# Who copies four partial sums out of PSUM: ScalarE or VectorE, in the gate and up projections of a streaming encoder layer

## The chip, the cores and the metric

The kernel runs on one core of a Trainium2 chip. The metric is the device time of one execution in microseconds (us); the median over runs is compared. A core has five engines that work side by side, each with its own in-order queue of instructions: TensorE (PE in the profile; the loading of its weights is shown apart as PEld), VectorE (DVE), ScalarE (ACT), GpSimd (POOL) and SyncE (SP, which here only starts DMAs). Matmuls add up into PSUM, which has eight banks; ScalarE and VectorE read the sums from there into SBUF. Weights come from HBM by DMA.

## The reference

One layer of a hybrid encoder for 320 positions (256 of a new stream, 64 of a running one) that share all weights: RMSNorm, one input projection, stick-breaking attention and a spatial gate, two branch projections, a merge, an output projection, and then the part that the change touches, the feed-forward network:

```
h = x + merged @ w_out[l]
hn = rmsnorm(h, norm_ffn[l])
gu = hn @ w_gate_up[l]
h = h + (jax.nn.silu(gu[..., :D_FF]) * gu[..., D_FF:]) @ w_down[l]
```

All is float32, with D_MODEL = 2048 and D_FF = 5632.

## The kernel before, in words

**Two numbers for one.** Every float32 weight is split in two: `wh`, the weight as ScalarE casts it to the fast matmul type, and `wl`, what is left of it, which VectorE gets by a subtraction (lines 70 and 71 in the projections before and after; lines 554 and 555 in the gate and up projections). Activations are split in the same way. A product then is high by high, high by low and low by high.

**The feed-forward network** goes over the 5632 hidden features in three slices of 16, 16 and 12 blocks of 128 (line 681). In a slice, `quad` (line 542) computes four blocks at a time, first for the gate half of the weights, then for the up half, so that there are 8, 8 and 6 quads, 22 in all; behind the quads of a slice the down projection for that slice runs (lines 687 to 698). Below, a quad for the gate half is a gate quad and one for the up half an up quad, and tile 0 to tile 7 are the eight pieces of weight (two rows of blocks by four columns, 512 KB each) that a quad loads.

**One quad** has two phases on TensorE:

- The main phase: for each of the eight tiles, SyncE loads `raw` (line 546; three buffers), ScalarE casts it into `wh` (line 554; four buffers), VectorE subtracts into `wl` or `low` (line 555; nine buffers, of which one quad uses eight), and ten matmuls 512 columns wide (line 562) use `wh` as the moving operand, 80 in all. They add up in three PSUM banks, `main`: the pool `acc` for a gate quad (three banks), the pool `aux` for an up quad (four banks). This result lies turned, with positions on the partitions.
- The low phase: four blocks b = 0 to 3 of 16 matmuls each (line 572), with the low parts of the weights as the stationary operand, each block summing in a bank of its own. Blocks 0 and 2 use the pool `aux1`, which has a single bank; blocks 1 and 3 take a bank of `aux`. **Line 573** copies the sum of a block (128 by 320) into the SBUF tile `total`, and so frees its bank. Block 2 can only begin when the copy of block 0 is done, as both use the one bank of `aux1`.

**Turning the main result** (`quad_turn`, line 580) is called ahead of the low phase: for each of the two 16-bit halves (planes) of the float32 numbers ScalarE makes three copies out of the `main` banks (line 587) and issues a transposing DMA (line 588). `quad_join` (line 591) is due some steps later: VectorE puts the two turned planes together (line 594, twice; the first needs both planes to have landed), adds them to `total` (lines 596 and 597), and then comes `gate_out` (lines 601 and 602) or `up_out` (lines 606 to 611).

**The order of the work** comes from a tile scheduler, which puts each engine's instructions in an order of its own from what it thinks they cost. It starts the casts and subtractions of the next quad inside the low phase of this one. `later` and `at` hold steps back until a given tick of the program; `quad_join` is due five ticks after the main phase.

**Who waits for whom.** A `raw` buffer is loaded again when both its cast and its subtraction are done. A `wl` or `low` buffer comes free when block 3 has used it, since block 3 is the last that reads it. So VectorE can subtract only one tile of the next quad before block 3 begins.

## Time and profile before

| what | value |
|---|---|
| median of three runs | 1700.63 us (1700.49 to 1702.84) |
| the profiled execution's own time | 1699.94 us |
| its span (first to last instruction) | 1698.2 us |
| TensorE busy | 1681.7 us, 99% |
| VectorE busy | 935.4 us, 55% |
| ScalarE busy | 769.4 us, 45% |
| granted TensorE clock, mean | 0.998 |

The profile is one execution. A row of a group tells the line, the engine, the operation, the tiles written and read, how many, their busy time, the mean of one in ns, and the idle time of that engine ahead of them with what ended it. A timeline row begins with the start and the length in us; xN says that N instructions are put together in it, and the brackets at its end show the idle time ahead of it and what released it. "ACTq" is the issuing of a DMA by ScalarE's queue.

### The profile page before, as it was taken

What the parts mean: (1) busy time and instruction counts of PE and PEld (TensorE: products, weight loads), DVE (VectorE), ACT (ScalarE), POOL (GpSimd) and SP (SyncE); (2) the same over time, 40 slices, a digit from 0 to 9 for tenths busy, and PEclk for the clock granted to TensorE, in tenths of its full rate; (3) what the DMA queues carried; (4) which work ended last, traced back from release to release, by engine and by line L of the source; (5) the groups of instructions that cost most, each with busy time, mean ns of one, the idle gap of its engine ahead of it and who ended that gap; (6) DMA issues with size and microseconds to landing.
All of it is one profiled execution on the core that took longest, in us unless ns stands there. A gap on an engine that the chain in (4) does not pass through costs nothing.

```text
span 1698.2 us, 25709 instructions
## 1 busy us (share of the span) xinstructions
PE 1681.7 (99%) x10496; PEld 1605.8 (95%) x10496; DVE 935.4 (55%) x1173; ACT 769.4 (45%) x1044; POOL 38.8 (2%) x68
## 2 busy tenths in 40 slices
PE   9999999999999999999999999999999999999998
PEld 9999999999999999998888899988888999888997
DVE  7665656544444445555555554446564644464666
ACT  7555645433333333445545532354555323545443
POOL 1100001000000000000000000000000000000000
PEclk9999999999999999999999999999999999999999
DMA  7866555444444444556666654566566545665554
GB/s 280 261 179 176 158 163 166 116 151 151 149 149 150 149 149 163 173 165 191 167 185 173 182 156 149 153 180 180 170 186 177 159 149 162 171 182 166 157 156 124
DMA packets 236983, 285.50 MB, mean 168 GB/s; under 512 B 98081, under 2 KB 194337, under 8 KB 236865
## 3 DMA queue, kind: packets, MB, share of 16 engines
q1 hardware_dynamic: 164016, 257.72, 48.5%
q10 hardware_dynamic: 70224, 17.88, 6.0%
q0 software_dynamic: 2624, 8.26, 1.6%
q8 instruction: 82, 1.34, 0.3%
q14 instruction: 37, 0.30, 0.0%
HBM read 256.03 MB, written 5.51 MB: 154 GB/s over the span
## 4 chain that ended last, share of the span: by engine, by line
PE 87%; DVE 5%; DMA 3%; ACT 3%; issue 2%; ACTq 0%; SPq 0%; DVEq 0%
PE acc L87 18%; PE acc L89 18%; PE acc L88 18%; PE aux L562 12%; PE aux L572 8%; PE acc L562 4%; DMA raw<-w_gu 3%; PE aux L89 2%; PE aux L88 2%; PE aux L87 2%; ACT flat L587 2%; DVE flat L594 1%; DVE wl L555 1%; DVE low L555 1%; ACT wh L554 1%
## 5 line engine op out<-in xcount | busy, mean ns | idle before, releaser
L70 ACT CAST wh<-raw 128x1024 fp32r<-128x1024 f32 (+2 forms) x296 | 302.7, 1023 | 542.8 <-PE acc L88 390.6
L71 DVE TENSOR_TENSOR wl<-raw,wh 128x1024 fp32r<-128x1024 f32 (+2 forms) x296 | 351.6, 1191 | 247.0 <-ACT wh L70 228.5
L87 PE MATMUL acc<-A,wh 128*128 128x320 f32 x1088 | 337.5, 310 | 0.5 <-ACT A L108 0.5
L88 PE MATMUL acc<-A,wh 128*128 128x320 f32 x1088 | 336.4, 309 | 0.0
L89 PE MATMUL acc<-A,wl 128*128 128x320 f32 x1088 | 336.2, 309 | 0.0
L554 ACT CAST wh<-raw 128x1024 fp32r<-128x1024 f32 x176 | 185.0, 1053 | 207.6 <-DMA raw<-w_gu 85.2
L87 PEld LDWEIGHTS acc<-A,wh 128*128 128x128 f32 x1088 | 204.3, 188 | 2.4 <-issue 1.5
L88 PEld LDWEIGHTS acc<-A,wh 128*128 128x128 f32 x1088 | 204.3, 188 | 0.3 <-DVE A L110 0.3
L89 PEld LDWEIGHTS acc<-A,wl 128*128 128x128 f32 x1088 | 204.2, 188 | 0.4 <-DVE wl L71 0.4
L562 PE MATMUL acc<-wh,A 128*128 128x512 f32 x880 | 201.6, 389 | 0.0
L562 PE MATMUL aux<-wh,A 128*128 128x512 f32 x880 | 201.5, 389 | 0.0
L555 DVE TENSOR_TENSOR low<-raw,wh 128x1024 fp32r<-128x1024 f32 x96 | 117.3, 1234 | 152.6 <-PE aux L572 121.6
L562 PEld LDWEIGHTS acc<-wh,A 128*128 128x128 f32 x880 | 164.7, 188 | 33.8
L562 PEld LDWEIGHTS aux<-wh,A 128*128 128x128 f32 x880 | 164.7, 188 | 33.7
L89 PE MATMUL acc<-act,wl 128*128 128x320 f32 x500 | 154.3, 309 | 0.7 <-DVE wl L71 0.7
L88 PE MATMUL acc<-act,wh 128*128 128x320 f32 x500 | 154.5, 309 | 0.0
L87 PE MATMUL acc<-act,wh 128*128 128x320 f32 x500 | 154.5, 309 | 0.0
L555 DVE TENSOR_TENSOR wl<-raw,wh 128x1024 fp32r<-128x1024 f32 x80 | 97.1, 1221 | 98.6 <-PE aux L572 75.5
L572 PE MATMUL aux<-A,low 128*128 128x320 f32 x768 | 130.6, 310 | 4.6 <-ACT sum L573 4.6
L572 PEld LDWEIGHTS aux<-A,low 128*128 128x128 f32 x768 | 117.2, 188 | 7.5 <-ACT sum L573 6.5
L572 PE MATMUL aux<-A,wl 128*128 128x320 f32 x640 | 110.4, 309 | 1.7 <-ACT sum L573 1.7
L572 PEld LDWEIGHTS aux<-A,wl 128*128 128x128 f32 x640 | 98.3, 188 | 2.9 <-ACT sum L573 2.2
(221 smaller groups left out, 2234.6 us busy)
## 6 DMA issues: line engine op xcount, KB each, us to landing
raw<-w_gu SPq DMA_DIRECT2D x176, 512.0 KB, 3.6
raw<-w_in SPq DMA_DIRECT2D x141, 512.0 KB, 3.7
raw<-w_down SPq DMA_DIRECT2D x80, 512.0 KB, 3.6
raw<-w_out SPq DMA_DIRECT2D x32, 512.0 KB, 3.6
raw<-w_a SPq DMA_DIRECT2D x16, 512.0 KB, 3.5
raw<-w_b SPq DMA_DIRECT2D x16, 512.0 KB, 3.5
raw<-w_down SPq DMA_DIRECT2D x16, 256.0 KB, 2.8
xr<-xT POOLq DMA_DIRECT2D x16, 160.0 KB, 2.5
```

The source lines that it names most:

```text
L70: nc.scalar.copy(out=wh[:, : n * P], in_=raw[:, : n * P])
L71: nc.vector.tensor_tensor(out=wl[:, : n * P], in0=raw[:, : n * P], in1=wh[:, : n * P].bitcast(F32), op=ALU.subtract)
L87: nc.tensor.matmul(ps[:, :T], a, x[0], start=first, stop=False)
L88: nc.tensor.matmul(ps[:, :T], a, x[1], start=False, stop=False)
L89: nc.tensor.matmul(ps[:, :T], b, x[0], start=False, stop=last)
L554: nc.scalar.copy(out=wh, in_=raw)
L555: nc.vector.tensor_tensor(out=wl, in0=raw, in1=wh.bitcast(F32), op=ALU.subtract)
L562: nc.tensor.matmul(main[i // 2].rearrange("p (b m) -> p b m", b=4), x[:, at0 : at0 + P], w, start=k == 0 and i % 2 == 0, stop=k == KD - 1 ...
L572: nc.tensor.matmul(ps[:, :T], lows[k // 2][:, at0 : at0 + P], hg[k][0], start=k == 0, stop=k == KD - 1)
L587: tc.keep_in_program_order(nc.scalar.copy(out=planes[:, i, c * 512 : (c + 1) * 512], in_=hw[:, :, 1 - i]))
L594: nc.vector.tensor_copy(rows[:, :, :, :, 1 - i], turned[:, i].rearrange("p (c b) t -> p b c t", c=3))
```

## The change

Line 573 alone is changed: the copy of a block's sum goes from ScalarE's queue to VectorE's.

```
@@ -570,7 +570,7 @@
             for k in range(KD):
                 at0 = (2 * b + k % 2) * P
                 nc.tensor.matmul(ps[:, :T], lows[k // 2][:, at0 : at0 + P], hg[k][0], start=k == 0, stop=k == KD - 1)
-            nc.scalar.copy(out=total[:, b, :], in_=ps[:, :T])
+            nc.vector.tensor_copy(total[:, b, :], ps[:, :T])
             tick()
         at(now + 5, quad_join, total, *turning)
```

There are 88 such copies, four in each of the 22 quads. The scheduler makes new orders for TensorE, ScalarE and VectorE from it, in the feed-forward part alone; the orders of GpSimd and SyncE stay as they are.

On TensorE, in the low phase of the third gate quad (the one whose main phase begins at 872.53 us in the profile of before; `aux_8779` is the bank of block 2, and `aux` stands for blocks 0, 1 and 3):

```order
 L572 MATMUL aux<-A,low 128x320 x8
 L572 MATMUL aux<-A,wl 128x320 x8
-L572 MATMUL aux<-A,low 128x320 x7
 L572 MATMUL aux_8779<-A,low 128x320 x8
 L572 MATMUL aux_8779<-A,wl 128x320 x8
-L572 MATMUL aux<-A,low 128x320
+L572 MATMUL aux<-A,low 128x320 x8
 L572 MATMUL aux<-A,wl 128x320 x8
```

Before, the scheduler put seven matmuls of block 3 ahead of block 2; now the blocks follow each other whole.

On ScalarE, from the up quad ahead of that gate quad's low phase to the low phase's end, before (`aux_8743` and `aux_8779` are the banks of blocks 0 and 2):

```order
L610 CAST act<-sum 128x320 x4
L554 CAST wh<-raw 128x1024 x4
L587 COPY flat<-acc 128x512 x3
L554 CAST wh<-raw 128x1024
L588 DMA_TRANSPOSE turned<-flat 128x12x128
L587 COPY flat<-acc 128x512 x3
L573 COPY sum<-aux_8743 128x320
L588 DMA_TRANSPOSE turned<-flat 128x12x128
L573 COPY sum<-aux 128x320
L573 COPY sum<-aux_8779 128x320
L573 COPY sum<-aux 128x320
L554 CAST wh<-raw 128x1024 x2
```

and the same place now:

```order
L610 CAST act<-sum 128x320 x4
L554 CAST wh<-raw 128x1024 x3
L587 COPY flat<-acc 128x512 x3
L554 CAST wh<-raw 128x1024
L588 DMA_TRANSPOSE turned<-flat 128x12x128
L587 COPY flat<-acc 128x512 x3
L554 CAST wh<-raw 128x1024
L588 DMA_TRANSPOSE turned<-flat 128x12x128
L554 CAST wh<-raw 128x1024 x3
```

The four copies are gone from it, and the first three copies of line 587 stand one cast earlier.

On VectorE, at the low phase of the up quad that follows (main phase from 901.12 us; `aux_8965` and `aux_9001` are the banks of its blocks 0 and 2), before:

```order
L555 TENSOR_TENSOR wl<-raw,wh 128x1024 x4
L555 TENSOR_TENSOR low<-raw,wh 128x1024 x2
L594 COPY flat<-turned 128x1536 x2
L555 TENSOR_TENSOR low<-raw,wh 128x1024
L596 TENSOR_TENSOR sum<-flat,sum 128x1280
L555 TENSOR_TENSOR low<-raw,wh 128x1024
L597 TENSOR_TENSOR sum<-flat,sum 128x4x64
```

and now:

```order
L573 COPY sum<-aux_8965 128x320
L573 COPY sum<-aux 128x320
L573 COPY sum<-aux_9001 128x320
L555 TENSOR_TENSOR low<-raw,wh 128x1024
L594 COPY flat<-turned 128x1536
L573 COPY sum<-aux 128x320
L594 COPY flat<-turned 128x1536
L555 TENSOR_TENSOR low<-raw,wh 128x1024
L596 TENSOR_TENSOR sum<-flat,sum 128x1280
L555 TENSOR_TENSOR low<-raw,wh 128x1024
L597 TENSOR_TENSOR sum<-flat,sum 128x4x64
L555 TENSOR_TENSOR low<-raw,wh 128x1024
```

Ahead of block 3's copy and of the second subtraction for the next quad there now stands the first line-594 copy, which waits for both turned planes.

More of the change, by code (lines that the diff above doesn't have):

```diff
@@ L572, in quad @@
                 nc.tensor.matmul(ps[:, :T], lows[k // 2][:, at0 : at0 + P], hg[k][0], start=k == 0, stop=k == KD - 1)
-            nc.scalar.copy(out=total[:, b, :], in_=ps[:, :T])
+            nc.vector.tensor_copy(total[:, b, :], ps[:, :T])
             tick()
```

## The prediction

> **What bounds the kernel now.** I read the page first, then the waits of the feed-forward stretch, then its timeline. The page:

> ```profile
> span 1698.2 us, 25709 instructions
> PE 1681.7 (99%) x10496; PEld 1605.8 (95%) x10496; DVE 935.4 (55%) x1173; ACT 769.4 (45%) x1044; POOL 38.8 (2%) x68
> ```

> TensorE is the bound, so a change that leaves the matmuls alone can win only its gaps. The waits from 770 to 1620 us (total, times, longest):

> ```profile
> PEld aux L572 <- ACT sum L573: 8.7, 9, 1.4
> PEld acc L89 <- DVE wl L71: 0.9, 1, 0.9
> DVE low L555 <- PE aux L572: 121.6, 16, 10.1
> DVE wl L555 <- PE aux L572: 75.5, 14, 10.1
> ```

> The weight loads wait nine times for line 573 and once for a subtraction, and for nothing else. VectorE stands still for up to 10.1 us at a time, until block 3 frees a low tile. One of the nine, in the gate quad at 872.53 us, on the timeline, with two phases of quads that have no wait, from the chain:

> ```profile
> 872.53 18.32 PE L562 MATMUL acc<-wh,A 128*128 128x512 f32 x80
> 891.38 1.05 ACT L554 CAST wh<-raw 128x1024 fp32r<-128x1024 f32 x1 [1.24 <-DMA raw<-w_gu]
> 892.33 1.55 ACT L587 COPY flat<-acc 128x512 uint16<-128x512 uint16 x3
> 893.76 1.07 ACT L554 CAST wh<-raw 128x1024 fp32r<-128x1024 f32 x1
> 893.91 1.46 ACTq L588 DMA_TRANSPOSE turned<-flat  x1
> 895.41 1.56 ACT L587 COPY flat<-acc 128x512 uint16<-128x512 uint16 x3 [0.58 <-ACT wh L554]
> 896.85 0.46 ACT L573 COPY sum<-aux 128x320 f32<-128x320 f32 x1
> 897.36 1.43 PE L572 MATMUL aux<-A,low 128*128 128x320 f32 x8 [0.79 <-ACT sum L573]
> 901.12 18.32 PE L562 MATMUL aux<-wh,A 128*128 128x512 f32 x80
> ```
> ```profile
> 845.16 18.16 PE aux L562 x80
> 975.43 9.38 PE aux L572 x64
> ```

> Undisturbed, a quad is 18.16 + 9.38 = 27.54 us; a low block is 9.38 / 4 = 2.35 us and a main tile 18.16 / 8 = 2.27 us. This quad took 901.12 - 872.53 = 28.59 us, 1.05 more. Its block 0 ended near 872.53 + 18.16 + 2.35 = 893.0, but the copy began at 896.85: ScalarE had a late cast, then line 587, a cast, the issue of the transposing DMA and line 587 again in front of it. TensorE did block 1 and the seven early matmuls of block 3, and then stood until the one bank of `aux1` was free.

> **What is removed.** The nine waits, 8.7 us. I count the weight loads' idle time and not that of the matmuls, since 1.05 us lost here is more than the 0.79 us in the matmul row: the first loads and matmuls behind a gap fill the pipeline again.

> **What is added.** 88 copies on VectorE. The trace has none on that engine; the nearest rows of 128x320 and of a like size are:

> ```profile
> L573 ACT COPY sum<-aux 128x320 f32<-128x320 f32 x88 | 38.3, 435 | 82.4 <-PE aux L572 82.4
> L671 DVE TENSOR_TENSOR h<-acc,h 128x320 f32<-128x320 f32 x26 | 12.8, 492 | 35.3 <-PE acc L89 35.3
> L597 DVE TENSOR_TENSOR sum<-flat,sum 128x256 f32<-128x256 f32 x22 | 9.3, 421 | 0.0
> ```

> So 0.42 to 0.49 us, and I take 0.45: line 671 reads PSUM with as many elements but has a second operand. [...]

> **Where the copies lie.** Copies 0, 1 and 2 fall into VectorE's standstill. Block 0 of the up quad at 901.12 ends at 921.63; VectorE's next row begins at 924.96 after 9.92 us of idling (below), so it is free from 915.04. Copy 0 is done by 922.4 and block 2 begins at 923.97: 1.5 us to spare, where ScalarE's copy came too late. Copy 3 and the new order cost something, as the first line-594 copy now stands ahead of copy 3 and of most subtractions for the next quad, and those free the `raw` buffers. What this does to the gate quad at 928.67, from these rows:

> ```profile
> 923.48 1.44 ACTq L588 DMA_TRANSPOSE turned<-flat  x1
> 924.96 1.23 DVE L555 TENSOR_TENSOR low<-raw,wh 128x1024 fp32r<-128x1024 f32 x1 [9.92 <-PE aux L572]
> 927.16 1.23 DVE L555 TENSOR_TENSOR low<-raw,wh 128x1024 fp32r<-128x1024 f32 x1 [0.97 <-PE aux L572]
> 928.31 1.98 DVE L594 COPY flat<-turned 128x1536 uint16<-128x1536 uint16 x2
> 928.67 16.51 PE L562 MATMUL acc<-wh,A 128*128 128x512 f32 x72
> 930.18 1.21 DVE L555 TENSOR_TENSOR low<-raw,wh 128x1024 fp32r<-128x1024 f32 x1
> 931.16 1.05 ACT L554 CAST wh<-raw 128x1024 fp32r<-128x1024 f32 x1 [1.86 <-PE acc L562]
> 931.31 1.48 DVE L596 TENSOR_TENSOR sum<-flat,sum 128x1280 f32<-128x1280 f32 x1
> 932.71 1.22 DVE L555 TENSOR_TENSOR low<-raw,wh 128x1024 fp32r<-128x1024 f32 x1
> ```
> ```profile
> raw<-w_gu SPq DMA_DIRECT2D x176, 512.0 KB, 3.6
> ```
> ```profile
> 1502.18 5.36 DMA raw<-w_gu
> ```
> ```profile
> DMA to landing us min/median/max: 3.6/3.7/5.4
> ```

> The last row is that of the transposing DMAs of line 588. Now, in the new order: block 3 runs from 926.32, its first tile is free after two matmuls and VectorE starts about 0.5 us later, so tile 1 is subtracted from 927.25 to 928.47 (before: 924.96, helped by block 3's early matmuls). The planes landed at 923.48 + 3.7 = 927.2, so line 594 runs to 929.5, copy 3 to 929.95, line 594 to 930.95, tile 2 to 932.15 (before: 928.39), line 596 to 933.5, tile 3 to 934.7 (before: 931.39), line 597 to 935.1, tile 4 to 936.3 (before: 933.93). Each subtraction lets SyncE load the tile three further on: 3.6 us to the landing, 5.36 at the longest in the chain, and 1.05 for the cast. Tile 5 is ready at 936.8 to 938.6 and TensorE wants it at 928.67 + 5 x 2.27 = 940.0; tile 6 at 939.4 to 941.1 for 942.3; tile 7 at 941.0 to 942.7 for 944.6. Between 1.2 and 3.2 us are left, so the cover holds: nothing. In the profile of before the cast at 931.16 waited for TensorE itself, which is where this slack shows. After a gate quad the new order has two subtractions ahead of copy 3, which is easier still. The low parts of tile 7 are wanted only in block 0, 20 us after the main phase begins.

> The chain does not build up from quad to quad, since VectorE waits again for block 3 in each. Moved on ScalarE: line 587 comes one cast earlier in most gate quads and loses nothing.

> **The one place that loses.** Behind the last quad of all VectorE has line 594 twice and then the first subtraction of the down projection, for which TensorE stands:

> ```profile
> 1599.56 1.99 DVE L594 COPY flat<-turned 128x1536 uint16<-128x1536 uint16 x2 [14.53 <-DMA turned<-flat]
> 1601.42 1.22 DVE L71 TENSOR_TENSOR wl<-raw,wh 128x1024 fp32r<-128x1024 f32 x1
> 1602.69 0.42 PE L89 MATMUL acc<-act,wl 128*128 128x320 f32 x1 [0.68 <-DVE wl L71]
> ```

> In the new order copy 2 stands between the two copies of line 594, so the subtraction comes 0.45 us later: +0.45. The other two slice ends have that first subtraction done ahead of copy 0, as before.

> **The sum**: -8.7 + 0.45 = -8.25 us. Against the profiled execution's own 1699.94 us (its span and 1.74 us around it) this is 1691.7. That execution lay 0.7 below the median of the runs, 1700.63, so for the median I say 1692.4.

> **The rivals.**

> *VectorE's queue starves the loads (slower).* The trace speaks for it in that VectorE is the fuller of the two engines. [...] As a mechanism: the planes land late, line 594 holds copy 3 and the subtractions, tile 6 comes late and TensorE stands in its main phase. It decides from the point where more than the 1.2 us left at tile 6 is gone, that is, where both planes land after about 930 instead of 927.2; the longest landing in the trace, 5.4 us, makes it 928.9. Eight gate quads follow an up quad inside a slice; if each stood 1.5 us, the sum were -8.25 + 12 = +3.75: 1704.4 for the median. Chance 0.09.

> *Copy 0 is late on VectorE too (part of the gain).* Tile 0 of the next quad is subtracted ahead of copy 0; by my times the queue shifts by 2 to 4 us and that subtraction ends about 1 to 3 us before block 0 does, with 2 us more until block 2 begins. If it fails in half of the nine, the gain is 8.25 - 4.35 = 3.9 us: 1696.7. Chance 0.12.

> *The wait only changes its owner (no change).* The third block waits for VectorE as long as it did for ScalarE, through something the trace does not show. Against it: VectorE has no work in that time. 1700.6. Chance 0.05.

> **How the numbers follow.** The forecast has 0.74, with its own range from 1690.8 (8.7 + 0.95, should the slice-end wait go as well, and 0.14 from the median to the lowest run) to 1694.5 (a quarter of the gain lost to small waits in the main phases). To hold 8 in 10 the range takes in the partial gain: 1690.8 to 1697.5. About 0.2%, 3.4 us, is what a measurement can tell from no change here; the partial gain straddles it, mostly above. Faster: 0.74 + 0.09 = 0.83. Same: 0.05 + 0.03 = 0.08. Slower: 0.09.

> **What would show it.** In the profile after, line 572 should wait for line 573 no more; every quad should take 27.54 us from one main phase to the next; copies 0 to 2 should sit in VectorE's idle time, 0.42 to 0.49 us each; casts of tiles 5 to 7 should come later than before but still wait mostly for TensorE; and the wait before line 89 at the last quad should grow from 0.95 to about 1.4 us. It is wrong if line 562 waits for line 554 (the first rival), or if line 572 still waits for line 573, now on VectorE (the second and third).

## The result, and the profile after

| | median | lowest to highest | runs |
|---|---|---|---|
| before | 1700.83 us | 1700.48 to 1702.97 | 10 |
| after | 1693.63 us | 1690.93 to 1701.08 | 10 |

The ratio is 0.9961 [0.9946, 0.9975]: faster by 7.2 us, where 1692.4 us was forecast. The new kernel is also less steady: its runs spread over 10 us, those of before over 2.5. Two later runs of the kernel before, which took 4293 and 4589 us, are left out of the medians below. The profiled execution took 1698.68 us, 5 us more than the median, so its trace shows what is given back near its largest.

The page of after:

```profile
span 1696.9 us, 25604 instructions
L573 DVE COPY sum<-aux 128x320 f32<-128x320 f32 x88 | 43.0, 489 | 157.8 <-PE aux L572 157.8
```

The work has moved as meant: VectorE is busy for 971.8 us in place of 935.4 and ScalarE for 734.1 in place of 769.4, a copy takes 489 ns on VectorE, and VectorE spent 157.8 us idle ahead of them, waiting for the blocks' sums. Now the waits between 770 and 1620 us (total, times, longest), after:

```profile
ACT wh L554 <- DMA raw<-w_gu: 259.9, 103, 8.3
DVE flat L594 <- DMA turned<-flat: 40.6, 18, 4.9
ACT wh L554 <- PE acc L562: 21.9, 15, 4.6
PEld acc L562 <- ACT wh L554: 3.5, 6, 1.0
PEld acc L89 <- DVE wl L71: 3.3, 2, 2.7
PEld aux L572 <- ACT flat L587: 1.4, 2, 1.0
```

and the three rows of before that the first three answer to:

```profile
ACT wh L554 <- DMA raw<-w_gu: 85.2, 51, 3.2
DVE flat L594 <- DMA turned<-flat: 19.4, 5, 14.5
ACT wh L554 <- PE acc L562: 54.7, 39, 3.3
```

The nine waits of line 572 for line 573 are gone; no row of that pair is left. Two new rows of the weight loads stand in their place, and the row of line 89 has grown from 0.9 to 3.3 us. One of the new ones is line 562 waiting for line 554: the mark that the prediction gave for its first rival. The casts wait for the weights three times as long as before and much less for TensorE, so the slack ahead of the main phases has shrunk. (That alone costs nothing: with the join later, below, they wait 219.3 us for the weights, and no main phase is longer.) Counted by the starts of all matmuls in that stretch, as far as they lie further apart than the undisturbed pace of their line, TensorE lost 8.8 us at line 572 and 1.2 at line 89 before, and now 1.4 at line 572, 2.5 at line 562 and 4.9 at line 89 with the matmuls right behind it: 10.0 against 8.9. The difference of 1.1 us agrees about with that of the spans, 1698.2 - 1696.9 = 1.3.

The place where it is given back shows best in the second slice. The timeline of VectorE after, only the first line-594 copy behind each quad:

```profile
1120.81 1.05 DVE L594 COPY flat<-turned 128x1536 uint16<-128x1536 uint16 x1
...
1150.21 1.06 DVE L594 COPY flat<-turned 128x1536 uint16<-128x1536 uint16 x1 [1.78 <-DMA turned<-flat]
...
1180.85 1.98 DVE L594 COPY flat<-turned 128x1536 uint16<-128x1536 uint16 x2 [3.34 <-DMA turned<-flat]
...
1208.43 1.07 DVE L594 COPY flat<-turned 128x1536 uint16<-128x1536 uint16 x1 [4.58 <-DMA turned<-flat]
```

The next main phases begin at 1121.41, 1148.95, 1176.49 and 1204.42 us. Against them the planes are put together at -0.60, +1.26, +4.36 and +4.01 us; before it was between -0.37 and +0.30 at all four. The delay grows over three quads and then stays near 4 us. (From the second quad of the first slice on it lies between 0.5 and 2.5 us, in the third between -0.2 and 1.7, and every quad inside these two takes 27.54 or 27.55 us.) The gate quad from 1204.42 then took 29.31 us in place of 27.54. A little later, at the gate quad from 1261.26, the timeline of all engines after shows the whole loop:

```profile
1253.57 1.05 ACT L554 CAST wh<-raw 128x1024 fp32r<-128x1024 f32 x1 [0.51 <-DMA raw<-w_gu]
1254.52 1.55 ACT L587 COPY flat<-aux 128x512 uint16<-128x512 uint16 x3
1256.06 1.05 ACT L554 CAST wh<-raw 128x1024 fp32r<-128x1024 f32 x1
1257.59 1.56 ACT L587 COPY flat<-aux 128x512 uint16<-128x512 uint16 x3 [0.48 <-ACT wh L554]
1259.18 1.43 ACTq L588 DMA_TRANSPOSE turned<-flat  x1
1261.26 17.23 PE L562 MATMUL acc<-wh,A 128*128 128x512 f32 x71
1264.73 1.05 DVE L594 COPY flat<-turned 128x1536 uint16<-128x1536 uint16 x1 [4.00 <-DMA turned<-flat]
1266.36 1.05 ACT L554 CAST wh<-raw 128x1024 fp32r<-128x1024 f32 x1 [7.21 <-DMA raw<-w_gu]
1266.99 1.22 DVE L555 TENSOR_TENSOR low<-raw,wh 128x1024 fp32r<-128x1024 f32 x1
1271.76 1.05 ACT L554 CAST wh<-raw 128x1024 fp32r<-128x1024 f32 x1 [4.35 <-DMA raw<-w_gu]
1272.86 2.17 PEld L562 LDWEIGHTS acc<-wh,A 128*128 128x128 f32 x10 [0.50 <-ACT wh L554]
```

Read it from the top: a cast that is late and waits for its weights stands ahead of both sets of line-587 copies (the cast between the sets stands there in the kernel before too), so the second plane's DMA is issued at 1259.18, 2.1 us ahead of the main phase instead of the 5.2 us of the prediction's quad. VectorE waits 4.00 us for it, with copy 3 and the subtractions queued behind. These subtractions come late, so the `raw` buffers are loaded late, ScalarE stands 7.21 and 4.35 us for weights, and TensorE for the cast. The casts of the next quad stand in ScalarE's queue ahead of the next line 587, and the circle closes. The DMA itself is slower too: in the six quads from 1148.95 us to the slice end the second plane took 5.0 to 6.1 us from issue to landing, where 3.7 is the median. At the gate quad from 1204.42 it landed 3.9 us into the main phase, at the same quad of before 1.5 us ahead of it; 3.7 us of the difference are the later issue and 1.7 the longer transfer.

### The profile page after: what moved, and what is told of

It reads as the page before. It is cut to its first block, busy times and chain, and to the rows that moved or that the text cites. A ratio compares the mean times of both kernels' runs of the same rounds, so it can differ in the third digit from the quotient of the medians.

```text
span 1696.9 us, 25604 instructions
## 1 busy us (share of the span) xinstructions
PE 1682.7 (99%) x10496; PEld 1607.0 (95%) x10496; DVE 971.8 (57%) x1261; ACT 734.1 (43%) x956; POOL 38.9 (2%) x68
## 4 chain that ended last, share of the span: by engine, by line
PE 87%; DMA 5%; DVE 4%; ACT 2%; issue 1%; ACTq 0%; SPq 0%; DVEq 0%
PE acc L89 18%; PE acc L87 18%; PE acc L88 18%; PE acc L562 9%; PE aux L572 8%; PE aux L562 7%; DMA raw<-w_gu 2%; DMA turned<-flat 2%; PE aux L89 2%; PE aux L88 2%; PE aux L87 2%; ACT flat L587 1%; DVE low L555 1%; DVE flat L594 1%; PE acc L639 1%
## 5 line engine op out<-in xcount | busy, mean ns | idle before, releaser
L71 DVE TENSOR_TENSOR wl<-raw,wh 128x1024 fp32r<-128x1024 f32 (+2 forms) x296 | 351.7, 1191 | 224.4 <-ACT wh L70 223.3
L89 PE MATMUL acc<-A,wl 128*128 128x320 f32 x1088 | 336.3, 309 | 0.0
L554 ACT CAST wh<-raw 128x1024 fp32r<-128x1024 f32 x176 | 185.3, 1054 | 317.8 <-DMA raw<-w_gu 259.9
L89 PEld LDWEIGHTS acc<-A,wl 128*128 128x128 f32 x1088 | 204.3, 188 | 0.2 <-DVE wl L71 0.2
L562 PE MATMUL acc<-wh,A 128*128 128x512 f32 x880 | 203.2, 390 | 1.1 <-ACT wh L554 1.0
L562 PE MATMUL aux<-wh,A 128*128 128x512 f32 x880 | 201.5, 389 | 0.0
L562 PEld LDWEIGHTS acc<-wh,A 128*128 128x128 f32 x880 | 164.2, 188 | 37.0 <-ACT wh L554 3.5
L562 PEld LDWEIGHTS aux<-wh,A 128*128 128x128 f32 x880 | 164.8, 188 | 33.7
L89 PE MATMUL acc<-act,wl 128*128 128x320 f32 x500 | 155.1, 311 | 2.8 <-DVE wl L71 2.8
L555 DVE TENSOR_TENSOR low<-raw,wh 128x1024 fp32r<-128x1024 f32 x96 | 117.8, 1235 | 37.4 <-ACT wh L554 37.1
L573 DVE COPY sum<-aux 128x320 f32<-128x320 f32 x88 | 43.0, 489 | 157.8 <-PE aux L572 157.8
L572 PE MATMUL aux<-A,low 128*128 128x320 f32 x768 | 128.6, 309 | 0.1
L572 PEld LDWEIGHTS aux<-A,low 128*128 128x128 f32 x768 | 117.1, 188 | 1.4 <-ACT flat L587 0.4
L555 DVE TENSOR_TENSOR wl<-raw,wh 128x1024 fp32r<-128x1024 f32 x80 | 97.6, 1224 | 22.1 <-ACT wh L554 22.1
L572 PE MATMUL aux<-A,wl 128*128 128x320 f32 x640 | 109.0, 309 | 0.8 <-ACT flat L587 0.8
## 6 DMA issues: line engine op xcount, KB each, us to landing
raw<-w_gu SPq DMA_DIRECT2D x176, 512.0 KB, 3.8
raw<-w_in SPq DMA_DIRECT2D x141, 512.0 KB, 3.7
raw<-w_down SPq DMA_DIRECT2D x80, 512.0 KB, 3.7
raw<-w_out SPq DMA_DIRECT2D x32, 512.0 KB, 3.6
raw<-w_a SPq DMA_DIRECT2D x16, 512.0 KB, 3.4
raw<-w_b SPq DMA_DIRECT2D x16, 512.0 KB, 3.5
```

The source lines that it names most:

```text
L71: nc.vector.tensor_tensor(out=wl[:, : n * P], in0=raw[:, : n * P], in1=wh[:, : n * P].bitcast(F32), op=ALU.subtract)
L89: nc.tensor.matmul(ps[:, :T], b, x[0], start=False, stop=last)
L554: nc.scalar.copy(out=wh, in_=raw)
L555: nc.vector.tensor_tensor(out=wl, in0=raw, in1=wh.bitcast(F32), op=ALU.subtract)
L562: nc.tensor.matmul(main[i // 2].rearrange("p (b m) -> p b m", b=4), x[:, at0 : at0 + P], w, start=k == 0 and i % 2 == 0, stop=k == KD - 1 ...
L572: nc.tensor.matmul(ps[:, :T], lows[k // 2][:, at0 : at0 + P], hg[k][0], start=k == 0, stop=k == KD - 1)
```

## The experiments

Two theories were set against each other. In short, A says that order decides: the gain comes from block 0's copy leaving the queue behind line 587, and what is given back comes from line 594 standing ahead of copy 3 and the subtractions while the planes are under way. B says that the amount of work on VectorE decides. (C and D, in the texts below, are rivals of single steps.) Each kernel ran beside the kernel before, whose medians were 1701.45 us (e1 to e4), 1701.19 (e5 to e8), 1702.41 (e9 to e11) and 1701.54 (e12).

**The join two ticks later.** As after, with `quad_join` and what follows it due later:

```
-        at(now + 5, quad_join, total, *turning)
+        at(now + 7, quad_join, total, *turning)
         for i in range(2):
-            at(now + 6 + i, done, total, 2 * i)
+            at(now + 8 + i, done, total, 2 * i)
```

> All four copies on VectorE as in the change, but quad_join and what follows it are due two ticks later, so that in every quad inside a slice the first line-594 copy stands behind copy 3 and two subtractions for the next quad. Theory A (the gain is the nine waits for line 573, 8.7 us; what is given back comes from line 594 standing ahead of the subtractions and holding the loads): the waits of line 562 and of line 572 for ScalarE go, 1690 to 1692, spread of the runs under 3 us; the stall ahead of line 89 at the last quad stays. Theory B (what is given back comes from VectorE having more work): as the change, 1693 to 1694, with the same spread of 10 us.

Measured: 1692.74 us (1691.9 to 1695.85), ratio 0.9952 [0.9939, 0.9965]. Waits in the same stretch:

```profile
DVE flat L594 <- DMA turned<-flat: 3.9, 2, 3.2
PEld acc L89 <- DVE wl L71: 1.9, 1, 1.9
```

The 40.6 us of waiting for planes are down to 3.9, and TensorE waits once in the whole stretch, at the slice end. VectorE at the main phase from 1204.09 us, with the same work:

```profile
1201.94 0.49 DVE L573 COPY sum<-aux 128x320 f32<-128x320 f32 x1 [1.85 <-PE aux L572]
1202.35 2.35 DVE L555 TENSOR_TENSOR low<-raw,wh 128x1024 fp32r<-128x1024 f32 x2
1204.62 0.48 DVE L573 COPY sum<-aux 128x320 f32<-128x320 f32 x1
1205.02 1.97 DVE L594 COPY flat<-turned 128x1536 uint16<-128x1536 uint16 x2
```

Two subtractions and copy 3 now stand ahead of line 594, which waits for nothing and begins 0.92 to 1.03 us into the next main phase all through the three slices, save at their ends. There is no build-up, and every quad takes 27.54 us. The order alone, with all 88 copies on VectorE, takes the loop away. One more run of this same kernel (its label names an edit that it doesn't have):

> The first run once more, one look: every quad at 27.54 us, a stall of 1.5 to 3 us ahead of line 89 at the last quad; 1691 to 1696.

Measured: 1691.94 us, with every quad between 27.54 and 27.58 us and 1.6 us of waiting ahead of line 89, as expected.

**All copies twice,** the join as in after (the second copy writes the same values again):

```
+            nc.vector.tensor_copy(total[:, b, :], ps[:, :T])
             nc.vector.tensor_copy(total[:, b, :], ps[:, :T])
```

> Every copy of line 573 is done twice in a row on VectorE: 88 more copies of 0.49 us, 43 us more work there, with line 594 early as in the change. Theory A: the added copies of blocks 0 to 2 fall into idle time and only the one of block 3 lengthens the queue ahead of the loads; 1692 to 1697, near the change. Theory B: what is given back doubles or more, 1697 to 1702.

Measured: 1710.78 us (1706.38 to 1713.9), ratio 1.005 [1.0038, 1.0061], slower than before and above what both theories allowed. Its waits (line 588 is line 587 here, and 595 is 594):

```profile
DVE flat L595 <- DMA turned<-flat: 45.3, 17, 5.3
PEld acc L562 <- ACT wh L554: 11.0, 12, 2.6
PEld acc L89 <- DVE wl L71: 6.5, 3, 4.1
```

They are the rows of after, grown. By itself this run can't tell order from work.

**All copies twice, the join later:**

> Every copy of line 573 done twice on VectorE as in the second run, but quad_join due two ticks later, so that line 594 stands behind two subtractions for the next quad. Theory A (the place of line 594 in VectorE's order decides): most of the loss goes, 1692 to 1697. Theory B (VectorE's added work decides): as the second run, 1707 to 1713.

Measured: 1695.2 us (1694.71 to 1700.55), ratio 0.9971 [0.996, 0.9982]. The same work as in the run before, 15.6 us faster. TensorE's only wait in the stretch:

```profile
PEld acc L89 <- DVE wl L71: 3.6, 1, 3.6
```

No main phase waits. Doubling the copies (43 us more on VectorE) costs 1695.2 - 1692.74 = 2.5 us, all of it at the last slice end as far as the trace shows. B falls: the same work costs little behind the right instructions and much ahead of them.

**Only blocks 1 and 3 on VectorE,** the join as in after:

```
-            nc.vector.tensor_copy(total[:, b, :], ps[:, :T])
+            if b % 2 == 1:
+                nc.vector.tensor_copy(total[:, b, :], ps[:, :T])
+            else:
+                nc.scalar.copy(out=total[:, b, :], in_=ps[:, :T])
```

> Only blocks 1 and 3 are copied by VectorE, blocks 0 and 2, whose bank is the single one of aux1, by ScalarE as before. Theory A: the waits of line 572 for line 573 stay, 6 to 9 us of them, so no gain: 1699 to 1703. Theory C (the gain comes from ScalarE having less to do, wherever the copies are): half of the gain, 1696 to 1697.

Measured: 1700.22 us (1699.07 to 1703.9), ratio 0.9993 [0.9985, 1.0002]. The waits of before are back, now for line 576:

```profile
PEld aux L572 <- ACT sum L576: 10.1, 10, 1.9
```

C fails: ScalarE has half of the copies less, and nothing is gained. Line 594 stands ahead of block 3's copy here too, with two subtractions for the next quad ahead of it as before, and no loop shows: inside the slices ScalarE issues the second plane 4.3 to 5.2 us ahead of the main phase, as before, and line 594 waits for planes once. So line 594 ahead of copy 3 does not start the loop by itself; how much of it hangs on the second subtraction and how much on ScalarE's new order is not shown.

**Only block 0 on VectorE, the join later** (`b == 0` in place of `b % 2 == 1`):

> Only block 0 is copied by VectorE (22 copies), the other three by ScalarE, and quad_join is due two ticks later, so that line 594 stands behind two subtractions. Theory A: the whole gain with a quarter of the copies, since block 2 waits for block 0's copy alone: 1690 to 1692. Theory C: a quarter of the gain, 1698 to 1699.

Measured: 1692.59 us (1692.03 to 1695.91), ratio 0.9948 [0.9936, 0.996]. One copy in four brings the whole gain, where C allowed a quarter of it. The other 66 bring nothing that these runs can tell.

**Is VectorE needed at all?** Three kernels keep all copies on ScalarE. The first leaves the second plane's line 587 and its DMA until block 0's copy has been issued, with the join later:

```
         turning = quad_turn(main)
+        turn_plane(main, 0, *turning)
         for b in range(4):
...
+            if b == 0:
+                turn_plane(main, 1, *turning)
```

`quad_turn` only makes the two tiles here, and `turn_plane` holds lines 587 and 588 for one plane.

> All four copies stay on ScalarE; the three line-587 copies of the second plane and its transposing DMA are issued behind block 0's copy instead of ahead of it, and quad_join is due two ticks later. Theory A (block 2 waited for the place of block 0's copy in ScalarE's queue, not for the engine): the wait goes without VectorE, 1690 to 1694. Theory D (ScalarE is too full in the low phase and only another engine helps): 1698 to 1702.

Measured: 1701.72 us (1699.91 to 1704.24), ratio 1.0003 [0.9994, 1.0012]. The expectation of A was missed. The timeline at the third gate quad shows why (line 592 is 587, 574 is 573, and 573 is 572):

```profile
891.82 1.05 ACT L554 CAST wh<-raw 128x1024 fp32r<-128x1024 f32 x1 [2.82 <-DMA raw<-w_gu]
892.77 1.55 ACT L592 COPY flat<-acc 128x512 uint16<-128x512 uint16 x3
894.37 1.05 ACT L554 CAST wh<-raw 128x1024 fp32r<-128x1024 f32 x1
894.39 1.46 ACTq L593 DMA_TRANSPOSE turned<-flat  x1
895.89 0.42 ACT L574 COPY sum<-aux 128x320 f32<-128x320 f32 x1 [0.47 <-ACT wh L554]
896.37 1.44 PE L573 MATMUL aux<-A,low 128*128 128x320 f32 x8 [0.96 <-ACT sum L574]
```

One set of copies is gone from in front of block 0's copy, but a cast that waited 2.82 us for its weights, the first set, another cast and the issue still stand there: the copy begins at 895.89 instead of 896.85. TensorE's order can be ruled out as the cause of the gain: its blocks follow each other whole in this kernel as they do after the change, and it still waits for ScalarE's copy:

```profile
PEld aux L573 <- ACT sum L574: 8.4, 9, 1.3
```

The second calls `quad_turn` whole behind block 0's copy, again with the join two ticks later:

> All four copies on ScalarE; both planes of line 587 and their transposing DMAs are issued behind block 0's copy, which so stands right behind the casts in ScalarE's queue; quad_join two ticks later, behind three subtractions. Theory A, as it stands after the sixth run (block 2 waits for what is queued ahead of block 0's copy, not for the engine): the waits of line 572 for the copy go, all or nearly, 1691 to 1695; a bank that line 587 frees later could cost 1 to 3 us of it. Theory D (only VectorE can do it): 1698 to 1702.

Measured: 1741.44 us (1737.79 to 1750.33), ratio 1.0241 [1.0217, 1.0265]. This was missed by far. The second plane now lands 0.8 to 9.2 us into the main phase inside the slices, and the loop runs without one copy on VectorE. But most of what TensorE loses, it loses in the low phases, to the late copy (line 571 is 572, 572 is 573, and 595 is 594):

```profile
PEld aux L571 <- ACT sum L572: 31.6, 14, 3.5
PEld aux L562 <- ACT wh L554: 8.1, 6, 2.2
```

The timeline around the start of the up quad at 909.61 us shows both:

```profile
903.40 1.04 ACT L554 CAST wh<-raw 128x1024 fp32r<-128x1024 f32 x1 [1.71 <-DMA raw<-w_gu]
904.35 0.42 ACT L572 COPY sum<-aux 128x320 f32<-128x320 f32 x1
...
917.99 1.99 DVE L595 COPY flat<-turned 128x1536 uint16<-128x1536 uint16 x2 [6.68 <-DMA turned<-flat]
...
927.49 3.09 PE L562 MATMUL aux<-wh,A 128*128 128x512 f32 x7 [1.82 <-ACT wh L554]
```

Block 0's copy stands behind a cast that waited 1.71 us for its weights, and TensorE, which had finished block 1, stood 2.11 us until 904.82. Then line 595 stands for 6.68 us with the subtractions behind it (the next begins at 921.49), and TensorE for 1.82 us in the middle of its main phase. So "behind block 0's copy" was not enough: the late casts stay ahead of that copy, and the later planes make the casts later still.

The third is before with the join later and the shift of the next paragraph:

> All four copies on ScalarE where they were before, with the two other edits of the eighth run: quad_join two ticks later, and the count shifted in the last slice. Theory A: the nine waits stay, only the 0.9 us ahead of line 89 go: 1699 to 1701. If the later quad_join were what makes the eighth run fast, 1690 to 1693.

Measured: 1701.55 us (1699.02 to 1706.31), ratio 1.0 [0.999, 1.001], with the waits for ScalarE's copy unchanged:

```profile
PEld aux L572 <- ACT sum L573: 8.4, 8, 1.8
```

So the two other edits together bring nothing that these runs can tell while block 0's copy is on ScalarE. Whether an order of ScalarE alone could do it stays open: no kernel here put block 0's copy ahead of the late casts, and D, which has it that only VectorE can, is not ruled out.

**The slice end.** A quad uses eight of nine low buffers in turn, four of them `wl` (which line 71 needs too) and five `low`. The last quad of the third slice leaves a `low` unused, those of the other two a `wl`. Moving the turn by four in the last slice makes it a `wl` there as well:

```
         act = []
+        if s0 + n == KF:
+            count[0] += 4
```

With all copies on VectorE and the join later:

> The first run (all copies on VectorE, quad_join two ticks later), and in the last slice the count that deals out the wl and low buffers begins four further on, so that a wl buffer is free for the first subtraction of the down projection, which then stands ahead of copy 0 and not behind line 594. Theory A: the stall ahead of line 89 at the last quad goes, 0.9 us against the kernel before and 1.9 or more against the first run: 1689.5 to 1691.5, and a narrower spread.

Measured: 1689.99 us (1689.68 to 1690.54), ratio 0.9935 [0.9923, 0.9947]. In the trace no wait of TensorE is left between 770 and 1620 us. With the join one tick later still:

> The eighth run with quad_join three ticks later in place of two, so that line 594 stands behind three subtractions. Theory A: no wait of TensorE is left in the quads for it to take away, so as the eighth run: 1689.5 to 1691. Rival: line 607 and the act tiles come later and the down projection or the buffers wait for them: 1692 or more.

Measured: 1689.92 us (1689.71 to 1690.07), ratio 0.9928 [0.9915, 0.994]: the same. With block 0's copy alone on VectorE and the join two ticks later:

> The fourth run (only block 0 copied by VectorE, quad_join two ticks later) with the shifted count in the last slice of the eighth. Theory A (22 copies, one per quad, carry the gain, and the other 66 do nothing for it): as the eighth run, 1689.5 to 1691. If the other three copies do something of their own, 1692 or more.

Measured: 1690.3 us (1689.9 to 1690.92), ratio 0.9931 [0.9916, 0.9946]: again the same, with one wait of 0.9 us (line 572 for line 587) left in its trace. These three are the best versions, faster than the kernel before beside them and than the median of the kernel after, and all their runs lie between 1689.68 and 1690.92 us.

## Why the prediction was right, and where it was not

- **The nine waits, -8.7 us: right.** The pair of lines 572 and 573 is gone from the waits after. Where nothing is given back in the main phases (join later) the gain is 1701.45 - 1692.74 = 8.7 us, although the slice end waits 1.9 us there in place of 0.9.
- **Copies 0 to 2 in VectorE's idle time, 0.42 to 0.49 us each: right.** 489 ns, the upper bound, and 157.8 us of idling ahead of them. The rival that copy 0 is late too didn't happen.
- **"So the cover holds: nothing": wrong,** and with it **"the chain does not build up from quad to quad".** The walk went through one quad and let the planes land at their time of before, 927.2 us. The time of the landing is itself set by the casts of the quad ahead, which stand in front of line 587 in ScalarE's queue. With line 594 in front of the subtractions a late landing makes late casts, and these make the next landing later. VectorE does stand still in each quad again, though for the sums of the blocks (157.8 us) and no longer for block 3 (0.2 us in place of 121.6 and 75.5); but the delay does not go through VectorE's start: it is carried on in ScalarE's queue. The sign that the casts would still wait mostly for TensorE failed with it (259.9 us for the weights, 21.9 for line 562 of the gate quads). In the profiled execution of after this cost 2.5 us in main phases, 1.4 us at line 572, and most of the growth at the slice end; the join two ticks later took the first two away without removing an instruction.
- **The first rival had the right place, but neither the threshold nor the size.** It was to decide from planes that land after 930 us, 1.33 us into the main phase. In the gate quads from 1204.42 and 1261.26 us line 594 began 4.01 and 3.47 us into it, and these two took 29.31 and 28.54 us. But in the gate quad from 815.96 us line 594 began at 818.05, 2.10 us into it, and TensorE didn't wait:

```profile
818.05 1.05 DVE L594 COPY flat<-turned 128x1536 uint16<-128x1536 uint16 x1 [2.62 <-DMA turned<-flat]
```

  So the point lay between 2.1 and 3.5 us here. The 1.2 us left at tile 6, from which the threshold came, goes by the longest load, 5.36 us; by the usual one of 3.6 us the same walk leaves 2.9. The rival was priced at eight quads by 1.5 us; two quads stood, by 1.8 and 1.0 us.
- **The last quad, +0.45 us: the row was right, the size too small.** The timeline of VectorE after:

```profile
1596.83 1.05 DVE L594 COPY flat<-turned 128x1536 uint16<-128x1536 uint16 x1 [3.93 <-DMA turned<-flat]
1597.78 0.47 DVE L573 COPY sum<-aux 128x320 f32<-128x320 f32 x1
1598.17 1.01 DVE L594 COPY flat<-turned 128x1536 uint16<-128x1536 uint16 x1
1599.07 1.21 DVE L71 TENSOR_TENSOR wl<-raw,wh 128x1024 fp32r<-128x1024 f32 x1
```

  Copy 2 stands between the two copies of line 594 as foretold. But the planes came late as well, so the wait grew from 0.9 to 2.7 us where 1.4 was forecast, and it was followed by 1.3 us that nobody had counted (below). The end of the second slice, which was to stay as it was, lost about 0.6 us ahead of line 89 as well.
- **The sum.** -8.25 us was forecast, and the medians give -7.2: the give-back of a typical execution is about one microsecond, that of the profiled one 8.25 - (1699.94 - 1698.68) = 7.0. The trace of an execution at the median was not seen, so how its loss is spread stays open, as does what sets off the loop more strongly in one execution than in another. That the forecast came within 1.2 us is therefore luck in part: it put nothing for the loop, and nothing in its working made the loop cheap in most runs. Three of the ten runs (1698.60, 1698.68 and 1701.08 us) lie above its range.
- **The kernels with the shift gain more than the 9.65 us of all waits in the trace of before:** 1701.19 - 1689.99 = 11.2 us. Between the lowest runs of the two it is 1699.61 - 1689.68 = 9.9 us, so most of the rest is that the runs of before spread upward by 4.5 us and theirs by 0.9. That this spread comes from the same queues is likely, but not shown.

## What to carry to other kernels

How full an engine is on average didn't decide here: what stands in front of an instruction in its queue did, and one copy in four carried the whole gain. Before moving work to another queue, look for an instruction there that waits for a DMA, and keep what frees the buffers for the next loads ahead of it. When walking through a cover of a microsecond or two, walk through two rounds and let each time that depends on the round before move with it.

## What the runs showed of the hardware that was not expected

**TensorE at half its clock after a short standstill.** Behind the wait at the last quad of after, one window of the trace (its length, then busy time and count of PE, PEld, DVE, ACT and POOL, then the granted clock, the DMA share and GB/s):

```profile
1600.30:1603.30 3.00, 2.97 (x11) 2.97 (x12) 3.00 (x4) 0.00 (x0) 0.00 (x0) 0.50 0.62 172
```

For 3 us the granted clock was 0.50, with 1.00 from 1590.0 to 1597.5 us and again from 1603.3 us to the last matmul, and the matmuls on the timeline began 0.26 us apart instead of the 0.15 of 1603.52 and 1603.66:

```profile
1600.33 0.64 PE L89 MATMUL acc<-act,wl 128*128 128x320 f32 x1 [2.39 <-DVE wl L71]
1600.77 0.47 PE L87 MATMUL acc<-act,wh 128*128 128x320 f32 x1
1601.03 0.47 PE L88 MATMUL acc<-act,wh 128*128 128x320 f32 x1
```

**The transposing DMAs beside the weight loads.** From issue to landing, line 588 takes 3.6 us at the least after the change, 3.7 as the median and 6.1 at the longest. The median is that of before, the longest 0.7 us more; with `quad_turn` behind the copy it reached 9.4 us at a median of 3.8. The long ones go with weight loads: of the 44 after, the five beside which loads of `raw` were under way for more than three quarters of the time took 5.0 to 6.1 us, and the other 39 took 3.7 as the median and 5.4 at the longest; before, no line 588 had loads beside it for more than 0.58 of its time. The prediction had taken 5.4, the longest of before, as the bound; the later ones of after fell beside more loads, and that bound did not hold.
